# Three moves in a two-block fp32 kernel: most SBUF tiles shifted by 64 bytes, two zeroings put at the head of a GpSimd chain, small VectorE chains cut into more pieces

## Chip, core and metric

The kernel runs as one program on one core of a Trainium2 chip. The metric is device time in microseconds (us) of one execution. The time before is 1152.12 us, the median of three runs (1150.99 to 1152.60).

## What is computed

Two transformer-like blocks over 256 positions of width 1024, in float32, one after the other. The part that matters here is the gated delta rule of the first block (8 heads, 128 wide, chunks of 64 in the reference; the kernel works it with chunks of 128):

```python
def first_block(x, ...):
    h = rmsnorm(x, norm_mix_g[l])
    proj = h @ w_in[l]
    bg, cg, xv, q, k, v, z, a, b, ga, gb = jnp.split(proj, pts, axis=-1)
    y_a = short_conv_branch(bg, cg, xv, conv_a_w[l]) @ w_a_out[l]
    y_b = gdn_branch(q, k, v, z, a, b, ...) @ w_b_out[l]
    mix = jax.nn.sigmoid(ga) * y_a + jax.nn.sigmoid(gb) * y_b
    x = x + mix @ w_o[l]
    h = rmsnorm(x, norm_ffn_g[l])
    x = x + conv_ffn(h, w_up[l], ffn_conv_w[l], w_down[l])
...
def gated_delta_rule_chunked(q, k, v, g, beta):
    G = jnp.cumsum(g, axis=-1)
    decay = jnp.exp(jnp.where(tril, G[..., :, None] - G[..., None, :], -jnp.inf))
    L = jnp.where(strict, jnp.einsum('bnhid,bnhjd->bnhij', k_beta, k) * decay, 0.0)
    sol = lax.linalg.triangular_solve(eye + L, rhs, left_side=True, lower=True)
    ...
    _, o = lax.scan(step, state0, xs)
```

The second block is attention in three dilated groups, a retention branch (a product of decayed scores with values) and a feed-forward part with a squared relu.

## The kernel before

**Jobs and units.** All dense products are cut into jobs of one 1 MB weight load each (`fm_job`, `tm_jobs`, `down_job`, `down2_job`). A job has two halves, called units here. In each unit the main loop does five things in this order: it advances the evacuations (`evs`), it splits the weights of the unit two ahead (`do_split`), it advances the evacuations again, it issues the unit's matmuls, and it advances the side chains (`auxes`) by one `yield` each. So a `yield` more in a side chain puts what follows it one unit later on every engine. The instruction order of each engine is fixed when the program is built; nothing is scheduled later.

**The split.** A float32 product is done as three passes in fp32r: weights are split into H (a ScalarE copy, line 143) and L = raw - H (a VectorE subtraction, line 146), activations likewise into a high and a low tile. A unit of `fm_job` has 24 matmuls (line 334): 128x128 weights from H or L stand still, and 256 columns of an activation tile (Hh, Hl, nh, nl, x2h, ...) are streamed past them. By the code there are 248 such units, 5,952 matmuls of 256 columns into the PSUM tiles named d; 47 of these units come before the inverse described below. `down_job` streams mh and ml past H and L into the PSUM tiles named x (528 matmuls of 256 columns). `tm_jobs` and `down2_job` do it the other way round: 512 columns of H or L are streamed past weights from x2h, x2l (624 matmuls) or mh, ml (384). The retention branch streams 512 columns of vrh, vrl past weights from a `w` tile (lines 325 to 327).

**Where tiles lie.** Each partition of SBUF holds, in this order: the raw weight buffers, the H and L buffers (from byte 41,088 on), the small constants, 15 large buckets of 8 KB (all activation tiles), the temporaries (`w` and others), and the mh/ml buffers. One of the constants is a tile `pad` of `LINE_PAD` floats that nothing reads. In the kernel before H, L, the buckets and mh/ml all start at a multiple of 128 bytes and the `w` tiles start 64 bytes beyond one. The warm-up at the program's start streams 256 columns of zeros whose first byte is 48, 56, 64 and 80 bytes beyond a multiple of 128 (8 matmuls each, list `WARM`), past weights that start at such a multiple.

**The delta rule's side chain.** `gates` computes the decay g with about 25 tiny VectorE operations (128x16 elements). `gdn_decay` sends g through DRAM and back as a 1 MB broadcast into the bucket gam (lines 501 and 502, issued by SP), waits `GAM_Y` units, and turns gam into the decay factors. `gdn_main` forms U (line 565 and what follows), sends its 32x32 diagonal blocks through DRAM into ebd, and queues `subst`. `subst` inverts the 64 small triangles by substitution on partitions 0 to 63: steps 31 to 24 on VectorE, 23 to 1 on GpSimd (line 146, tiles bt and ebd). Then it writes the result and its transpose to DRAM (lines 600 and 602, GpSimd's queue), zeroes the buckets Em, Dm and P (lines 603, 605, 608, GpSimd), waits `SC_Y` units, scatters the blocks into Em and Dm (line 614: block rows 0 and 2 from GpSimd's queue, 1 and 3 from SP's), waits `SC_Z` units and sets `sub_ok`. After that `gdn_main` starts the inverse on TensorE (line 663 reads Dm), between units of dense work. SP also issues all weight loads (line 316), in order; a load waits until its raw buffer is free, and so does everything behind it.

Of the kernel before, what the change touches and what calls it, by code (L numbers as in the profile page):

```python
# [8 lines left out]
I32 = mybir.dt.int32  # L9
# [3 lines left out]
MUL, ADD, SUB = ALU.mult, ALU.add, ALU.subtract  # L13
# [3 lines left out]
D = 1024  # L17
RAW_BUFS = 3
N_BUCKETS = 15
LINE_PAD = 8  # L20
HL_BUFS = 3
W_BUFS = 6
WARM = ([(0, 0, 512, 0)] * 11 + [(128 * i, 1024 + d, 256, i % 2) for d in (12, 14, 16, 20) for i in range(8)])
# [2 lines left out]
DG, DV, DQ = 1, 0, 3  # L26
AT_Y = 5
SQ_Y = 1
GAM_Y = 4
ORDER = ((0,), (1,), (2,))  # L30
D1_Q = 2
SG_Y = {8: 3, 0: 4, 16: 5}
U_Y = 1
SC_Y = 2
SC_Z = 4
EXP1 = 1


# [60 lines left out]
def _build(tc, nc, A, ACT, DVE, POOL, PE, SP, raw_p, hl_p, c_p, b_p, t_p, m_p, s_p, d_p, x_p):  # L99
    uid = [0]  # L100

    def nm(s):
        uid[0] += 1
        return f"{s}{uid[0]}"
# [4 lines left out]
    def alloc(shape, dt=F32, what="bk"):  # L109
        if not free_tags:  # L110
            raise RuntimeError(f"no bucket for {what} at {cur}: {len(tag_of)}")
        tag = free_tags.pop()
        t = b_p.tile([128] + list(shape), dt, tag=tag, name=nm(what))
        tag_of[id(t)] = (tag, t)
        return t

    def free(*ts):
        for t in ts:
            free_tags.insert(0, tag_of.pop(id(t))[0])

    def tmp(tag, shape=(2, 256), dt=F32, bufs=None):
        return t_p.tile([128] + list(shape), dt, tag=tag, name=nm(tag), **({"bufs": bufs} if bufs else {}))

    def cst(name, shape, dt=F32):
        return c_p.tile(list(shape), dt, tag=name, name=name)

    def psx(shape=(512,)):
        t = x_p.tile([128, 512], F32, tag="x", name=nm("x"))
        return shaped(t, shape)
# [12 lines left out]
    def act(out, in_, func, **kw):  # L142
        ACT.activation(out=out, in_=in_, func=func, **kw)  # L143

    def tt(eng, out, a, b, op):
        eng.tensor_tensor(out=out, in0=a, in1=b, op=op)  # L146

    def stt(out, in0, scalar, in1, op0, op1):
        DVE.scalar_tensor_tensor(out=out, in0=in0, scalar=scalar, in1=in1, op0=op0, op1=op1)  # L149

    def ts(out, in0, s1, op0, s2=None, op1=None):
        if s2 is None:
            DVE.tensor_scalar(out=out, in0=in0, scalar1=s1, scalar2=None, op0=op0)
        else:
            DVE.tensor_scalar(out=out, in0=in0, scalar1=s1, scalar2=s2, op0=op0, op1=op1)
# [8 lines left out]
    def pts(out, in0, s1, op0, s2=None, op1=None):  # L164
        if s2 is None:
            POOL.tensor_scalar(out=out, in0=in0, scalar1=s1, scalar2=None, op0=op0)
        else:
            POOL.tensor_scalar(out=out, in0=in0, scalar1=s1, scalar2=s2, op0=op0, op1=op1)

    def rsqrt(y, v, n, steps=3, dve=False):  # L170
        a = tmp(f"nw{n}", (n,))
        DVE.tensor_scalar(out=y.bitcast(I32), in0=v.bitcast(I32), scalar1=-0.5, scalar2=float(0x5F3759DF), op0=MUL, op1=ADD)
        for _ in range(steps):
            if dve:
                tt(DVE, a, y, y, MUL)
                stt(a, a, -0.5, v, MUL, MUL)
                stt(y, a, 1.5, y, ADD, MUL)
                continue
            tt(POOL, a, y, y, MUL)
            tt(POOL, a, a, v, MUL)  # L180
            pts(a, a, -0.5, MUL, 1.5, ADD)
            tt(POOL, y, y, a, MUL)
# [28 lines left out]
    DVE.memset(warm[:, 512:2048].bitcast(F32), 0.0)  # L211
    cst("pad", [128, LINE_PAD])
    eps = cst("epsc", [128, 1])
# [193 lines left out]
    gd = {}  # L407
# [21 lines left out]
    def gates():  # L429
        ps = psx((2, 16))  # L430
        for c in range(2):
            PE.matmul(ps[:, c, :], lhsT=gd["ab"][:, 128 * c:128 * c + 128], rhs=gd["id2"], start=c == 0, stop=c == 1, skip_group_check=True)
        yield
        def sm(n): return cst(n, [128, 2, 8])
        bet, xx, na, u, m, s, s2, p, g = (sm(n) for n in ("bet", "sx", "sna", "su", "smx", "ss_", "ss2", "spp", "gg"))
        gd["bet"], gd["g"] = bet, g
        act(bet, ps[:, :, 8:16], AF.Sigmoid)
        tt(DVE, xx, ps[:, :, 0:8], adt[:, 1:2, :].to_broadcast([128, 2, 8]), ADD)
        stt(na, xx, -1.0, xx, MUL, ALU.min)
        nA = cst("nA", [128, 1, 8])  # L440
        act(nA[:, 0, :], adt[:, 0, :], AF.Exp)
        act(u, na, AF.Exp)
        yield
        ts(m, xx, 0.0, ALU.max)
        ts(s, u, 2.0, ADD)
        DVE.reciprocal(out=s, in_=s)
        yield
        fl = lambda t: t.rearrange("p a b -> p (a b)")
        tt(DVE, fl(s), fl(s), fl(u), MUL)
        tt(DVE, fl(s2), fl(s), fl(s), MUL)  # L450
        ts(fl(p), fl(s2), 1.0 / 17, MUL, 1.0 / 15, ADD)
        yield
        for k in range(6, -1, -1):
            tt(DVE, fl(p), fl(p), fl(s2), MUL)
            ts(fl(p), fl(p), 1.0 / (2 * k + 1), ADD)
            if k in (2, 4):
                yield
        ts(fl(s), fl(s), -2.0, MUL)
        tt(DVE, fl(p), fl(p), fl(s), MUL)
        tt(DVE, fl(p), fl(p), fl(m), SUB)  # L460
        for c in range(2):
            tt(DVE, g[:, c, :], p[:, c, :], nA[:, 0, :], MUL)
        yield
        yield
        yield from gdn_decay()
        yield from gdn_main()

    def gdn_norm_k():
# [15 lines left out]
    def gdn_decay():  # L484
# [17 lines left out]
        SP.dma_start(out=gam.rearrange("p a b -> p (a b)"), in_=gs.rearrange("a b -> (a b)").partition_broadcast(128))  # L502
        for _ in range(GAM_Y):
            yield
# [48 lines left out]
    def gdn_main():  # L553
        ks, sums = gd["ks"], gd["sums"]
        kt0, St = ks[:, 0], ks[:, 1]
        rq, sq = gd["rq"], gd["sq"]
# [24 lines left out]
        def subst():  # L581
            ef = eb.rearrange("p r c -> p (r c)")
            POOL.memset(ef, 0.0)
            POOL.memset(ef[:, 0:1024:33], 1.0)
            for _ in range(3):
                yield
            def step(eng, i):
                w = 32 - i
                t = tmp("bt", (256,))[0:64, 0:i * w].rearrange("p (r c) -> p r c", c=w)
                tt(eng, t, blk[:, 0:i, i:i + 1].to_broadcast([64, i, w]), eb[:, i:i + 1, i:32].to_broadcast([64, i, w]), MUL)  # L590
                tt(eng, eb[:, 0:i, i:32], eb[:, 0:i, i:32], t, SUB)

            for i in range(31, 0, -1):
                step(POOL if i < 24 else DVE, i)
                if i % (2 if 7 < i < 24 else 4) == 0:
                    yield
            for _ in range(SUB_W):
                yield
            gd["Em"], gd["Dm"] = alloc([16, 128], what="Em"), alloc([16, 128], what="Dm")
            POOL.dma_start(out=d2.rearrange("b u r c -> (b u) r c"), in_=eb)  # L600
            POOL.tensor_copy(out=blk, in_=eb.rearrange("p r c -> p c r"))
            POOL.dma_start(out=d3.rearrange("b u r c -> (b u) r c"), in_=blk)
            POOL.memset(gd["Em"], 0.0)
            yield
            POOL.memset(gd["Dm"], 0.0)
            yield
            gd["P"] = alloc([16, 128], what="P")
            POOL.memset(gd["P"], 0.0)
            for _ in range(SC_Y):
                yield  # L610
            for dd, dst in ((d2, gd["Em"]), (d3, gd["Dm"])):
                for b in range(4):
                    bs = slice(32 * b, 32 * b + 32)
                    (POOL, SP)[b % 2].dma_start(out=dst[bs, :, bs], in_=dd[b].rearrange("u r c -> r u c"))
            free(ebd)
            for _ in range(SC_Z):
                yield
            gd["sub_ok"] = True

        auxes.append((subst(), ()))  # L620
        while "q_ok" not in gd:
            yield
# [20 lines left out]
        free(gam, KQ[0])  # L643
        yield
        ts(sq, sq, EPS, ADD)
        rsqrt(rq, sq, 16, dve=True)
        rq2 = cst("rq2", [128, 16])
        ts(rqs, rq, 128 ** -0.5, MUL)
        tt(DVE, rq2, rqs, rqs, MUL)
# [2 lines left out]
        Em, Dm, P = gd["Em"], gd["Dm"], gd["P"]  # L652
# [137 lines left out]
        S["ob"] = (Oh, Ol)  # L790

    jobs.append(Job(load_w("w_in", 0, 8, 7168, 128), ab_mm, ab_evac, halves=1, start=(gates,), split=ab_split))
    for p in range(4):
        fm_job("w_in", 4096 + 256 * p, "x", qkv_evac(K, 8, p), start=(gdn_keys,) if p == 3 else ())
# [871 lines left out]
```

## Time and profile before

| | us |
|---|---|
| median of 3 runs | 1152.12 |
| the profiled execution, its own time | 1150.97 |
| its span, first to last instruction | 1149.2 |
| TensorE busy (matmul) | 1127.2 |
| VectorE busy | 750.5 |
| ScalarE busy | 586.0 |
| GpSimd busy | 241.7 |
| mean granted TensorE clock | 0.991 |

The span is 1.8 us shorter than the execution's own time. Matmuls are pipelined and the ends of their rows are modelled, so the spacing of their starts says more than their durations. In rows, `d<-Hh,L` means: into PSUM tile d, streamed tile Hh, standing weights L. A release in brackets names what ended the idle time ahead of a row.

### The profile page before, as it was taken

Reading aid. Unit: us, or ns where it says so; the run is one execution under the profiler, and the core shown is the slowest. Engines: PE = TensorE matmul, PEld = TensorE weight load, DVE = VectorE, ACT = ScalarE, POOL = GpSimd, SP = SyncE. Lnnn points to the kernel's source line nnn. Section 1 sums busy time; section 2 is a strip of 40 time slices with the busy share of each in tenths; the row PEclk is TensorE's granted clock in tenths of the full one; section 3 lists DMA queues with packets and bytes.
Section 4 is the critical chain, followed back from the end, with each engine's and each line's share of the span. In section 5 each row is a group of like instructions: output and inputs, shape, how many; then the busy total and the mean of one; then the engine's idle time right before and its main releaser. Section 6 shows DMA issues by size and latency. Waiting matters only on the chain.

```text
span 1149.2 us, 20224 instructions
## 1 busy us (share of the span) xinstructions
PE 1127.2 (98%) x8340; PEld 1073.6 (93%) x8340; DVE 750.5 (65%) x1033; ACT 586.0 (51%) x944; POOL 241.7 (21%) x245
## 2 busy tenths in 40 slices
PE   9899897999999999999999999999999999999998
PEld 8899897999999999999878899889999999899997
DVE  4957984344577987778854566556685558655554
ACT  6776253256554444444678554555474445444442
POOL 2565696010401221222200500001340001000000
PEclk9999998999999999999999999999999999999999
DMA  8455366243554555555575544453436555555552
GB/s 258 147 164 186 111 193 174 75 146 112 182 186 150 181 188 183 192 178 178 183 250 190 184 146 147 139 191 113 163 129 220 184 184 168 176 191 189 190 187 74
DMA packets 155087, 194.82 MB, mean 170 GB/s; under 512 B 5678, under 2 KB 132005, under 8 KB 154740
## 3 DMA queue, kind: packets, MB, share of 16 engines
q1 hardware_dynamic: 153888, 191.57, 51.1%
q0 software_dynamic: 912, 1.43, 0.5%
q8 instruction: 65, 1.06, 0.4%
q10 hardware_dynamic: 196, 0.54, 0.1%
q14 instruction: 26, 0.21, 0.0%
HBM read 191.68 MB, written 1.84 MB: 168 GB/s over the span
## 4 chain that ended last, share of the span: by engine, by line
PE 84%; POOL 5%; DVE 4%; ACT 3%; DMA 2%; issue 2%; POOLq 0%; DVEq 0%; ACTq 0%
PE d L334 63%; PE x L334 13%; POOL bt L146 2%; POOL ebd L146 2%; DVE L L146 2%; ACT jk L143 1%; ACT H L143 1%; DVE w L149 1%; DMA Dm<-scr 1%; POOL gam L146 1%; PE x L663 0%; PE x L1181 0%; PE x L1206 0%; DMA scr<-U 0%; DMA xtm<-in_x_dram 0%
## 5 line engine op out<-in xcount | busy, mean ns | idle before, releaser
L146 DVE TENSOR_TENSOR L<-raw,H 128x1024 fp32r<-128x1024 f32 x354 | 443.2, 1258 | 256.8 <-ACT H L143 253.2
L143 ACT ACTIVATE H<-raw 128x1024 fp32r<-128x1024 f32 (+1 forms) x355 | 369.9, 1053 | 205.2 <-PE d L334 152.4
L334 PE MATMUL d<-Hh,L 128*128 128x256 f32 x576 | 82.2, 286 | 6.2 <-DVE L L146 6.2
L334 PE MATMUL d<-Hh,H 128*128 128x256 f32 x576 | 85.6, 292 | 0.7 <-ACT H L143 0.7
L334 PE MATMUL d<-nh,H 128*128 128x256 f32 x608 | 85.9, 283 | 0.0
L334 PE MATMUL d<-nl,H 128*128 128x256 f32 x608 | 85.7, 283 | 0.0
L334 PE MATMUL d<-nh,L 128*128 128x256 f32 x608 | 85.7, 283 | 0.0
L334 PEld LDWEIGHTS d<-Hh,L 128*128 128x128 f32 x576 | 74.7, 193 | 7.4 <-DVE L L146 7.4
L334 PE MATMUL d<-Hl,H 128*128 128x256 f32 x576 | 81.2, 284 | 0.0
L334 PEld LDWEIGHTS d<-nh,H 128*128 128x128 f32 x608 | 79.2, 191 | 1.2
L334 PEld LDWEIGHTS d<-nh,L 128*128 128x128 f32 x608 | 78.6, 192 | 0.0
L334 PEld LDWEIGHTS d<-nl,H 128*128 128x128 f32 x608 | 78.5, 192 | 0.0
L334 PEld LDWEIGHTS d<-Hh,H 128*128 128x128 f32 x576 | 75.2, 194 | 1.4 <-ACT H L143 0.9
L334 PEld LDWEIGHTS d<-Hl,H 128*128 128x128 f32 x576 | 74.9, 193 | 0.0
L334 PE MATMUL d<-H,x2h 128*128 128x512 f32 x208 | 56.9, 396 | 1.0 <-ACT H L143 1.0
L334 PE MATMUL d<-x2h,H 128*128 128x256 f32 x384 | 55.8, 288 | 0.0
L334 PE MATMUL d<-H,x2l 128*128 128x512 f32 x208 | 55.7, 390 | 0.0
L334 PE MATMUL d<-L,x2h 128*128 128x512 f32 x208 | 55.7, 390 | 0.0
L334 PE MATMUL d<-x2h,L 128*128 128x256 f32 x384 | 53.9, 283 | 0.0
L334 PE MATMUL d<-x2l,H 128*128 128x256 f32 x384 | 53.9, 283 | 0.0
L334 PEld LDWEIGHTS d<-x2h,H 128*128 128x128 f32 x384 | 49.8, 190 | 0.6
L334 PEld LDWEIGHTS d<-x2h,L 128*128 128x128 f32 x384 | 49.5, 191 | 0.0
(402 smaller groups left out, 1922.8 us busy)
## 6 DMA issues: line engine op xcount, KB each, us to landing
raw<-in_w_in_dram SPq DMA_DIRECT2D x86, 1024.0 KB, 5.1
raw<-in_w_up_dram SPq DMA_DIRECT2D x38, 1024.0 KB, 5.3
raw<-in_w_down_dram SPq DMA_DIRECT2D x27, 1024.0 KB, 4.8
raw<-in_w_proj_b_dram SPq DMA_DIRECT2D x8, 1024.0 KB, 5.1
raw<-in_w_a_out_dram SPq DMA_DIRECT2D x4, 1024.0 KB, 6.1
raw<-in_w_b_out_dram SPq DMA_DIRECT2D x4, 1024.0 KB, 5.3
raw<-in_w_o_dram SPq DMA_DIRECT2D x4, 1024.0 KB, 6.0
raw<-in_w_out_dram SPq DMA_DIRECT2D x4, 1024.0 KB, 5.2
```

Of the source, the lines that this page charges most:

```text
L143: ACT.activation(out=out, in_=in_, func=func, **kw)
L146: eng.tensor_tensor(out=out, in0=a, in1=b, op=op)
L149: DVE.scalar_tensor_tensor(out=out, in0=in0, scalar=scalar, in1=in1, op0=op0, op1=op1)
L334: PE.matmul(out, lhsT=x if swap else w, rhs=w if swap else x, start=first and ps == 0, stop=last and ps == group[-1] and group is (order o ...
```

## The change

Five edits. `LINE_PAD` goes from 8 to 24 floats, so that every tile behind `pad` moves up by 64 bytes: the buckets and mh/ml now start 64 bytes beyond a multiple of 128, the `w` tiles at a multiple; raw, H and L stay. The zeroing of Em and Dm moves from behind the substitution to its head, with its two `yield`s; `SC_Z` goes from 4 to 6. In `gates` the loop yields at four places instead of two; `GAM_Y` goes from 4 to 2. The reciprocal root of the query norms is written out with a `yield` after each of its three rounds.

```diff
-LINE_PAD = 8
+LINE_PAD = 24
-GAM_Y = 4
+GAM_Y = 2
-SC_Z = 4
+SC_Z = 6
         for k in range(6, -1, -1):
             tt(DVE, fl(p), fl(p), fl(s2), MUL)
             ts(fl(p), fl(p), 1.0 / (2 * k + 1), ADD)
-            if k in (2, 4):
+            if k in (1, 2, 4, 5):
                 yield
...
             POOL.memset(ef, 0.0)
             POOL.memset(ef[:, 0:1024:33], 1.0)
-            for _ in range(3):
-                yield
+            gd["Em"], gd["Dm"] = alloc([16, 128], what="Em"), alloc([16, 128], what="Dm")
+            for k in ("Em", "Dm"):
+                POOL.memset(gd[k], 0.0)
+                yield
+            yield
...
             for _ in range(SUB_W):
                 yield
-            gd["Em"], gd["Dm"] = alloc([16, 128], what="Em"), alloc([16, 128], what="Dm")
             POOL.dma_start(out=d2.rearrange("b u r c -> (b u) r c"), in_=eb)
             POOL.tensor_copy(out=blk, in_=eb.rearrange("p r c -> p c r"))
             POOL.dma_start(out=d3.rearrange("b u r c -> (b u) r c"), in_=blk)
-            POOL.memset(gd["Em"], 0.0)
-            yield
-            POOL.memset(gd["Dm"], 0.0)
-            yield
             gd["P"] = alloc([16, 128], what="P")
...
         ts(sq, sq, EPS, ADD)
-        rsqrt(rq, sq, 16, dve=True)
+        a = tmp("nw16", (16,))
+        DVE.tensor_scalar(out=rq.bitcast(I32), in0=sq.bitcast(I32), scalar1=-0.5, scalar2=float(0x5F3759DF), op0=MUL, op1=ADD)
+        for _ in range(3):
+            tt(DVE, a, rq, rq, MUL)
+            stt(a, a, -0.5, sq, MUL, MUL)
+            stt(rq, a, 1.5, rq, ADD, MUL)
+            yield
```

On VectorE, the end of `gates` (spp and its neighbours are the tiny tiles, L the weight splits that TensorE waits for, w a convolution). Before:

```order
L146 TENSOR_TENSOR spp<-spp,ss_342 128x16
L153 TENSOR_SCALAR spp<-spp 128x16
L146 TENSOR_TENSOR spp<-spp,ss_342 128x16
L153 TENSOR_SCALAR spp<-spp 128x16
L153 TENSOR_SCALAR ss__341<-ss__341 128x16
L146 TENSOR_TENSOR spp<-spp,ss__341 128x16
L146 TENSOR_TENSOR spp<-spp,smx 128x16
L146 TENSOR_TENSOR gg<-spp,nA 128x8 x2
L146 TENSOR_TENSOR L_580<-raw_303,H_579 128x1024
L146 TENSOR_TENSOR L_617<-raw_403,H_616 128x1024
```

In the change:

```order
L146 TENSOR_TENSOR spp<-spp,ss_342 128x16
L153 TENSOR_SCALAR spp<-spp 128x16
L146 TENSOR_TENSOR L_610<-raw_403,H_609 128x1024
L149 SCALAR_TENSOR_TENSOR w_603<-d_535,prm,w_603 128x254 x2
L149 SCALAR_TENSOR_TENSOR w_603<-d_535,prm,w_603 128x253 x2
L146 TENSOR_TENSOR spp<-spp,ss_342 128x16
L153 TENSOR_SCALAR spp<-spp 128x16
L153 TENSOR_SCALAR ss__341<-ss__341 128x16
L146 TENSOR_TENSOR spp<-spp,ss__341 128x16
L146 TENSOR_TENSOR spp<-spp,smx 128x16
L146 TENSOR_TENSOR gg<-spp,nA 128x8 x2
L146 TENSOR_TENSOR L_659<-raw_403,H_658 128x1024
```

The nine tiny operations that stood ahead of L in one run now have a split and a convolution between them, seven remain together, and gg is complete two units later.

On GpSimd, the end of `subst`. Before:

```order
L600 DMA scr_1284<-ebd_1290 64x1024
L601 COPY ebd_1290<-ebd_1290 64x1024
L602 DMA scr_1285<-ebd_1290 64x1024
L603 MEMSET Em_1992 128x2048
L605 MEMSET Dm_1993 128x2048
L608 MEMSET P_2062 128x2048
L614 DMA Em_1992<-scr_1284 32x16x32 x2
L614 DMA Dm_1993<-scr_1285 32x16x32 x2
```

In the change:

```order
L602 DMA scr_1284<-ebd_1290 64x1024
L603 COPY ebd_1290<-ebd_1290 64x1024
L604 DMA scr_1285<-ebd_1290 64x1024
L606 MEMSET P_1999 128x2048
L612 DMA Em_1342<-scr_1284 32x16x32 x2
L612 DMA Dm_1343<-scr_1285 32x16x32 x2
```

Two zeroings are gone from between the substitution's result and its scatters; they now stand right behind lines 583 and 584, ahead of the first substitution step on GpSimd.

On SP, the same place. Before:

```order
L316 DMA raw_2002<-in_w_in_dram 128x8x256
L316 DMA raw_2068<-in_w_a_out_dram 128x8x256
L614 DMA Em_1992<-scr_1284 32x16x32 x2
L614 DMA Dm_1993<-scr_1285 32x16x32 x2
L316 DMA raw_2146<-in_w_a_out_dram 128x8x256
```

In the change:

```order
L316 DMA raw_2005<-in_w_in_dram 128x8x256
L612 DMA Em_1342<-scr_1284 32x16x32 x2
L612 DMA Dm_1343<-scr_1285 32x16x32 x2
L316 DMA raw_2076<-in_w_a_out_dram 128x8x256
L316 DMA raw_2146<-in_w_a_out_dram 128x8x256
```

SP's scatters now stand ahead of the first load of `w_a_out`. The inverse itself (line 663) starts behind the same unit as before, the 48th: two units fewer for the zeroings, two more from `SC_Z`.

## Rows read from the trace of the kernel before

**Rows 1.** The page, part 1: busy time, share of the span, instructions.

```profile
PE 1127.2 (98%) x8340; PEld 1073.6 (93%) x8340; DVE 750.5 (65%) x1033; ACT 586.0 (51%) x944; POOL 241.7 (21%) x245
```

**Rows 2.** Waits of TensorE's matmul queue over the whole span: engine, tile, line, whom it waited for, us in total, times, longest.

```profile
PE x L663 <- DMA Dm<-scr: 7.9, 1, 7.9
PE d L334 <- DVE L L146: 6.2, 6, 2.4
...
```

**Rows 3.** Busy time by stretch: us, then busy (instructions) of PE, PEld, DVE, ACT, POOL, then the granted TensorE clock, DMA share, GB/s.

```profile
188.00:210.00 22.00, 22.00 (x148) 20.81 (x147) 10.78 (x16) 5.47 (x7) 7.95 (x5) 0.79 0.31 97
572.00:975.00 403.00, 402.02 (x2808) 376.63 (x2808) 251.46 (x326) 220.71 (x366) 47.20 (x51) 1.00 0.52 172
```

**Rows 4.** Instructions of TensorE in order of time, around its waits: start us, us, and in brackets the idle time ahead and its releaser.

```profile
40.37 1.22 PE L334 MATMUL d<-Hh,L 128*128 128x256 f32 x8 [0.70 <-DVE L L146]
...
49.08 1.22 PE L334 MATMUL d<-Hh,L 128*128 128x256 f32 x8 [2.27 <-DVE L L146]
...
51.26 2.08 PE L334 MATMUL d<-Hh,H 128*128 128x256 f32 x8
...
138.86 1.89 PE L334 MATMUL d<-Hh,L 128*128 128x256 f32 x8 [2.40 <-DVE L L146]
...
187.40 3.65 PE L663 MATMUL x<-Dm,U 128*128 128x64 f32 x16 [7.92 <-DMA Dm<-scr]
190.80 2.06 PE L334 MATMUL d<-yah,H 128*128 128x256 f32 x8
...
194.09 1.12 PE L334 MATMUL d<-yah,L 128*128 128x256 f32 x8
```

**Rows 5.** Instructions of VectorE in order of time, 36 to 49 us, the end of `gates`.

```profile
44.19 0.16 DVE L146 TENSOR_TENSOR spp<-spp,ss 128x16 f32<-128x16 f32 x1
...
47.81 2.35 DVE L146 TENSOR_TENSOR L<-raw,H 128x1024 fp32r<-128x1024 f32 x2
```

**Rows 6.** Instructions of VectorE and of SP's queue in order of time, 50 to 82 us: the way of gam.

```profile
56.63 0.27 DVE L498 COPY gr<-x 16x128 f32<-16x128 f32 x1
...
58.47 0.34 SPq L502 DMA_DIRECT2D gam<-gs  x1
...
64.11 0.68 DVE L549 COPY ks<-x 128x512 f32<-128x512 f32 x1
...
70.91 1.28 DVE L146 TENSOR_TENSOR gam<-gam,cmats 128x512 f32<-128x512 f32 x2
```

**Rows 7.** Instructions of GpSimd in order of time, 95 to 192 us.

```profile
122.96 0.59 POOL L146 TENSOR_TENSOR bt<-ebd 64x207 f32<-64x207 f32 x1 [8.94 <-DVE ebd L146]
...
172.16 0.54 POOL L602 DMA_DIRECT2D scr<-ebd  x1 [0.30 <-POOL ebd L601]
172.69 1.82 POOL L603 MEMSET Em<- 128x2048 f32 x1
174.43 1.82 POOL L605 MEMSET Dm<- 128x2048 f32 x1
...
179.26 1.29 POOL L614 DMA_DIRECT2D Dm<-scr  x2
```

**Rows 8.** SP's queue in order of time, 163 to 181 us.

```profile
163.06 0.37 SPq L316 DMA_DIRECT2D raw<-in_w_a_out_dram  x1
...
177.22 1.05 SPq L316 DMA_DIRECT2D raw<-in_w_a_out_dram  x2
```

**Rows 9.** DMA issues by tensor: issuing queue, count, KB each, median us from issue to landing.

```profile
raw<-in_w_in_dram SPq DMA_DIRECT2D x86, 1024.0 KB, 5.1
...
raw<-in_w_a_out_dram SPq DMA_DIRECT2D x4, 1024.0 KB, 6.1
...
scr<-ebd POOLq DMA_DIRECT2D x2, 256.0 KB, 2.9
...
Dm<-scr SPq DMA_DIRECT2D x2, 64.0 KB, 2.4
...
Dm<-scr POOLq DMA_DIRECT2D x2, 64.0 KB, 7.4
```

**Rows 10.** The chain that ended last, whole span: start us, us, what. These pieces are gapless runs of matmuls, so length over count is their spacing.

```profile
395.10 11.52 PE d L334 x96
...
406.61 5.70 PE x L334 x48
...
846.66 120.95 PE d L334 x1008
...
1088.83 5.58 PE x L334 x24
```

**Rows 11.** Instructions of TensorE in order of time: the end of the warm-up, 512-column streams past x2l, and the retention product.

```profile
6.16 3.96 PE L271 MATMUL d<-warm 128*128 128x256 f32 x32
9.96 0.27 PE L250 MATMUL d<-cmats,prr 128*128 128x128 f32 x1
...
592.64 1.07 PE L334 MATMUL d<-H,x2l 128*128 128x512 f32 x4
...
596.26 1.07 PE L334 MATMUL d<-L,x2h 128*128 128x512 f32 x4
...
783.22 0.39 PE L325 MATMUL x<-vrh,w 128*128 128x512 f32 x1
...
785.28 0.88 PE L334 MATMUL d<-x2h,H 128*128 128x256 f32 x6
```

## The prediction

> **What bounds the kernel now.** I read the page's busy times first: TensorE's matmul queue is busy for 1127.2 us of the 1149.2 us span, VectorE for 65%, GpSimd for 21% [rows 1]. So almost the whole time is matmul spacing, and a saving is either a wait of TensorE that goes or a closer spacing. The list of TensorE's waits comes next: one of 7.9 us for the DMA into Dm, and 6.2 us in six waits for the weight split L on VectorE [rows 2]. The instructions around them [rows 4] show the waits at 40.4, 49.1, 138.9 and 187.4 us. A wait can also cost clock: 8 matmuls take 2.06 us in the row at 190.80 and 1.12 us in the row at 194.09, where the clock is back. [...] So the five edits split into two groups: the side chains can only change what happens before about 190 us, and the 64 bytes can change the spacing everywhere.
>
> **The change part by part: zeroing.** GpSimd ends the substitution's writes with the DMA at 172.16, zeroes Em, Dm and P, then issues its scatters, Dm's last [rows 7]. The zeroings start 1.74 us apart (172.69, 174.43), so without two of them the Dm scatters issue 3.5 us earlier, at 175.8 instead of 179.26. They read what the DMA of 172.16 writes, and such writes land in 2.9 us [rows 9], at 175.0: that holds nothing back. At their new place the zeroings take 3.5 us of GpSimd while VectorE does steps 31 to 24; GpSimd sits idle there for 8.94 us [rows 7]. That cover is enough, so they cost nothing. If it were gone, they would cost the same 3.5 us and the edit would be void. TensorE's wait ends when the last Dm scatter lands, so the resumption moves by **-3.5 us**.
>
> **Scatter and loads.** GpSimd's Dm scatters take 7.4 us to land, SP's only 2.4 [rows 9]; GpSimd's were issued 2 us behind two 1 MB loads on SP at 177.22 [rows 8]. In the change SP's scatters wait for the data landing at 175.0, and three loads stand right behind, among them the one that used to go at 163.06 [rows 8]. GpSimd's Dm scatters at 175.8 thus still meet loads. I take 7.4 again, which is the row of the same queue beside loads: **0 us**, with a gain of up to 5.0 us if they landed as SP's do. The moved load issues near 175.8 instead of 163.06, lands 6.1 us later [rows 9] at 181.9, and is split some 2.4 us later, if ScalarE's copy takes no more than VectorE's 1.2 us (two L in 2.35 us [rows 5]), by 184.3. Its first matmuls stand behind 16 inverse matmuls of 3.65 us [rows 4] that now start near 183.9, so they would be asked for at 187.6: covered by 3.4 us. If the scatters did land in 2.4 us, this cover would cap the gain at about 4.6.
>
> [...]
>
> **Gates in more pieces.** The tiny operations from 44.19 to 47.8 us push L to 47.81 [rows 5], and TensorE waits 2.27 us for it; the earlier wait of 0.70 us has the same source [rows 4]. With the row at 51.26 (2.08 against 1.12) about 1.0 us of clock, and some 0.3 behind it, hang on the longer one. All of it is 4.3 us. The pieces now stand between splits, but seven operations stay together at the end. The price is that gr, at 56.63, moves two units on, to where the second ks copy stood, 64.11 [rows 6]. The 1 MB gam transfer then issues near 66 instead of 58.47; in before's time its first use, at 70.91, does not move since `GAM_Y` loses two units. A 1 MB load lands in 5.1 us [rows 9], so gam would land near 71: no cover is left, and a late gam holds VectorE and the splits queued behind it, for which TensorE waits. I take **-2.5 us** that reach the scatter chain, between 0 (gam eats it) and -4.3.
>
> **Root in three pieces.** Twelve tiny operations ahead of L cost TensorE the 2.40 us at 138.9 and some clock after [rows 4]. This lies before the wait for Dm, whose end GpSimd's chain sets, not TensorE. What TensorE saves there it waits longer at 187.4: **0 us**, and up to 4 if that chain stopped being the last. So the side chains give -3.5 - 2.5 = -6.0 us, between 0 and -12.5.
>
> **The 64 bytes.** TensorE is busy for 98% of the span [rows 1], so it is on spacing that they can act in bulk. Read from gapless runs: the d products with 256 columns, streamed tile and weights both at a multiple of 128, have 120.95/1008 = 119.99 ns and 11.52/96 = 120.0; the x products past mh, also both at 0, 5.70/48 = 118.75 [rows 10]. The nearest to the new state is the warm-up, streamed 48 to 80 bytes beyond: from 6.16 to 9.96 us 32 matmuls, 118.75 ns [rows 11]. With 512 columns: 226.3 ns past x2l and x2h (592.64 to 596.26, 16 matmuls, both at 0), 5.58/24 = 232.5 past mh [rows 10], and 228.9 in the retention product (783.22 to 785.28, 9 matmuls), whose `w` weights lie 64 bytes off the streamed vr tiles [rows 11]. So where 64 bytes are already in the kernel, 256 columns are 1.25 ns closer than now, and 512 columns 2.6 ns wider than one neighbour and 3.6 closer than the other. For the 512-column products I take 0. For the 4,824 matmuls of 256 columns into d behind the inverse I take the warm-up's row, since it has their shape and the same PSUM pattern: 4,824 x 1.25 ns = **-6.0 us**. The bounds are 0 and -2.5 ns on one side (-12 us), and the retention row's +2.6 ns on the other.
>
> The sum: 1150.97 - 6.0 - 6.0 = 1139.0 for the profiled execution. The median of the runs is 1.15 us above that execution, so I forecast **1140.1 us**.
>
> **The rivals.**
> - *The spacing does not depend on where tiles lie.* Then the 118.75 of the x products is a matter of PSUM tiles, and that of the warm-up of its zeros. For it: x and d differ with both at 0. Against it: the warm-up uses d tiles like the 120 ns runs. Only -6.0 remains: 1146.1. [...]
> - *The 64 bytes widen the spacing, as in the retention row.* At +2.6 ns on 4,824 matmuls of d, 528 of the x products and 1,008 of 512 columns, 6,360 in all, this is +16.5 us, net +10.5: 1162.6, slower than before. It decides from 6.0 us / 6,360 = 0.94 ns per matmul on. For it: that row has exactly the new distance. Against it: its other 512-column neighbour is wider still.
> - *The wait for Dm does not end earlier,* because GpSimd's scatters stay behind the loads that now stand closer, or gam arrives late. Then only the spacing counts: 1146.1. For it: 7.4 against 2.4 us shows how loads hold scatters; against it: they held them before as well.
> - *The scatters land early too:* -4.3 - 3.5 - 4.6 with the spacing's -6.0 gives 1133.7.
>
> **How the numbers follow.** The forecast has 43%, unmoved spacing 24%, wider spacing 15%, an unmoved wait 9%, early scatters 9%. The range 1130 to 1149 takes in all but the wider spacing and the far ends, about 2 in 10. About 0.2% (2.3 us) is what a measurement of this kernel can tell from no change. Faster by more: 43 + 9, 20 of the 24, 6 of the 9 and 1 of the 15, 79%. Within: 4 + 3 + 1 = 8%. Slower: 13%.
>
> **What would show it.** In the profile after, Dm's zeroing stands near 114 to 118 us and no longer near 174; GpSimd's last scatter issues some 6 us earlier and the inverse starts near 181; the wait there may be as long as before. The waits at 40 and 49 us are gone or under 1 us, and none appears at gam near 68. A d run of 1008 matmuls takes 119.7 us instead of 120.95. I am wrong if that run is 120.9 or longer, if line 663 starts after 185, or if a new wait stands behind gam.

## The result and the profile after

| | before | after |
|---|---|---|
| median of 4 runs, us | 1152.30 | 1134.52 |
| range of the runs, us | 1150.99 to 1152.60 | 1133.89 to 1136.21 |
| span of the profiled execution, us | 1149.2 | 1132.1 |
| start of the inverse (line 663, now 667), us | 187.40 | 181.35 |
| from there to the end, us | 961.8 | 950.75 |

The ratio is 0.985, with a 95% interval of 0.9833 to 0.9867: the change makes the kernel 17.8 us faster. The two last lines of the table split the profiled executions' 17.1 us: 6.05 us come before the inverse, 11.05 us behind it. The page's first part, as [rows 1]:

```profile
PE 1111.5 (98%) x8340; PEld 1054.7 (93%) x8340; DVE 754.4 (67%) x1033; ACT 584.8 (52%) x944; POOL 242.0 (21%) x245
```

TensorE's busy time is 15.7 us less for the same 8340 matmuls, and its share is still 98%: it is again the spacing that fills the time. Next TensorE's waits over the whole span, as [rows 2] (waiting tile and line, whom it waited for, us in total, times, longest):

```profile
PE d L334 <- DVE L L146: 6.8, 7, 2.5
PE x L667 <- DMA Dm<-scr: 6.0, 1, 6.0
```

The waits have moved more than they have shrunk. TensorE's instructions around them, as [rows 4]:

```profile
46.12 1.21 PE L334 MATMUL d<-Hh,L 128*128 128x256 f32 x8 [0.65 <-DVE L L146]
...
53.44 1.21 PE L334 MATMUL d<-Hh,L 128*128 128x256 f32 x8 [0.95 <-DVE L L146]
...
77.00 1.22 PE L334 MATMUL d<-Hh,L 128*128 128x256 f32 x8 [1.18 <-DVE L L146]
...
139.34 1.21 PE L334 MATMUL d<-Hh,L 128*128 128x256 f32 x8 [2.50 <-DVE L L146]
...
181.35 3.65 PE L667 MATMUL x<-Dm,U 128*128 128x64 f32 x16 [6.00 <-DMA Dm<-scr]
184.75 2.05 PE L334 MATMUL d<-yah,H 128*128 128x256 f32 x8
```

The waits behind `gates` (0.70 and 2.27 us before) are 0.65 and 0.95 us, and no row of 2.08 us follows. A new wait of 1.18 us stands at 77.00. The 2.40 us behind the root are 2.50 us one unit later. On VectorE the source of the new wait is seen: it stood idle 2.03 us for gam.

```profile
69.40 1.29 DVE L146 TENSOR_TENSOR gam<-gam,cmats 128x512 f32<-128x512 f32 x2 [2.03 <-DMA gam<-gs]
```

GpSimd's instructions, as [rows 7]:

```profile
113.31 1.81 POOL L587 MEMSET Dm<- 128x2048 f32 x1
120.79 0.59 POOL L146 TENSOR_TENSOR bt<-ebd 64x207 f32<-64x207 f32 x1 [5.67 <-DVE ebd L146]
...
170.18 0.55 POOL L604 DMA_DIRECT2D scr<-ebd  x1 [0.30 <-POOL ebd L603]
170.71 1.83 POOL L606 MEMSET P<- 128x2048 f32 x1
...
173.80 1.29 POOL L612 DMA_DIRECT2D Dm<-scr  x2
```

The zeroings lie in idle time, 5.67 us of which are still left, and the Dm scatters follow the last write by 3.62 us instead of 7.10. The gapless runs of the chain that ended last, as [rows 10] (start, us, what):

```profile
381.88 5.45 PE x L334 x48
...
797.73 24.49 PE d L334 x216
...
834.20 118.72 PE d L334 x1008
...
1106.00 5.51 PE x L334 x24
```

Length over count: x past mh with 256 columns 113.5 ns (118.75 before), d 117.8 ns in the long run (120.0 before), but 113.4 in the run of 216, and the 512 columns past mh 229.6 ns (232.5 before). The 512 columns past x2 went the other way, 2.80 us for the 12 matmuls between the first and the last of these rows, 233.3 ns (226.3 before):

```profile
572.42 1.10 PE L334 MATMUL d<-L,x2h 128*128 128x512 f32 x4
573.35 1.10 PE L334 MATMUL d<-H,x2h 128*128 128x512 f32 x4
574.28 1.09 PE L334 MATMUL d<-H,x2l 128*128 128x512 f32 x4
575.22 1.09 PE L334 MATMUL d<-L,x2h 128*128 128x512 f32 x4
```

The sum behind the inverse is thus 4,824 x -2.21 - 528 x 5.25 + 624 x 7.0 - 384 x 2.9 ns = -10.2 us, against -11.05 measured. Three things in the traces are not in it. Over a run of 240, before and after, the 512 columns past x2 widened by 6.3 ns and not 7.0 (228.1 to 234.4), which makes the sum -10.6:

```profile
588.84 54.74 PE d L334 x240
...
576.84 56.26 PE d L334 x240
```

The d runs at 113.3 to 113.5 ns (the 216, 48 each at 677.09 and 693.14, and 24 at 792.95) bring some 1.5 us more. And the first 24 matmuls of d behind the wait for Dm, before and after, took 0.7 us longer: the granted clock over them was 0.67 before (190.80 to 195.20 us) and 0.54 after (184.75 to 189.70).

```profile
191.04 4.17 PE d L334 x24
...
185.00 4.88 PE d L334 x24
```

Together that is -11.4 us; the last 0.3 us stay open.

### The profile page after: what moved, and what is told of

Same layout as the page of the kernel before. It is cut to its first block, busy times and chain, and to the rows that moved or that the text cites. A ratio compares the mean times of both kernels' runs of the same rounds, so it can differ in the third digit from the quotient of the medians.

```text
span 1132.1 us, 20217 instructions
## 1 busy us (share of the span) xinstructions
PE 1111.5 (98%) x8340; PEld 1054.7 (93%) x8340; DVE 754.4 (67%) x1033; ACT 584.8 (52%) x944; POOL 242.0 (21%) x245
## 4 chain that ended last, share of the span: by engine, by line
PE 83%; POOL 5%; DVE 5%; DMA 2%; ACT 2%; issue 2%; DVEq 0%; ACTq 0%; POOLq 0%
PE d L334 62%; PE x L334 13%; POOL ebd L146 2%; POOL bt L146 2%; DVE L L146 2%; ACT jk L143 1%; ACT H L143 1%; DVE w L149 1%; DMA Dm<-scr 1%; PE x L667 0%; PE x L1185 0%; PE x L1210 0%; DMA scr<-U 0%; DMA xtm<-in_x_dram 0%; PE x L669 0%
## 5 line engine op out<-in xcount | busy, mean ns | idle before, releaser
L334 PE MATMUL d<-Hh,H 128*128 128x256 f32 x576 | 82.9, 285 | 0.6 <-ACT H L143 0.6
L334 PEld LDWEIGHTS d<-Hh,H 128*128 128x128 f32 x576 | 72.6, 188 | 1.1 <-ACT H L143 0.8
L143 ACT ACTIVATE w<-w 128x512 f32<-128x512 f32 (+1 forms) x35 | 21.7, 619 | 51.8 <-POOL w L146 19.9
```

The lines of the kernel that those rows point to most:

```text
L334: PE.matmul(out, lhsT=x if swap else w, rhs=w if swap else x, start=first and ps == 0, stop=last and ps == group[-1] and group is (order o ...
```

## The experiments

All times are medians of their runs, and ratios are to the kernel before, run on the same chip. Numbers 8, 11 and 12 are single runs; only the spacing in their traces is read.

**1. The pad alone.** The kernel before with

```diff
-LINE_PAD = 8
+LINE_PAD = 24
```

> The kernel before with LINE_PAD 24 and nothing else. Theory (the spacing follows from where the tiles lie): the same spacing as in the changed kernel, 117.75 ns for d, 113.5 ns for x past mh, 233 ns for 512 columns past x2, 229 past mh. Behind the inverse that is 4,824 x -2.25, 528 x -5.2, 624 x +6.3 and 384 x -3 ns, -10.8 us, and some 1.8 us more because TensorE reaches the delta rule sooner (about 800 matmuls of d before 104 us): 1139.7 us. [...]

Measured: 1141.43 us, ratio 0.9913 (0.9896 to 0.9929). The spacing is that of the changed kernel: 117.8 ns for d (118.72 us for the run of 1008) and 113.5 for x past mh (5.45 us for 48). From the inverse to the end it is 949.8 us, 12.0 less than before. The inverse did not start sooner but 2.4 us later: GpSimd's scatters were issued 1.2 us later and took 8.7 us to land instead of 7.4 (the last one 8.60 instead of 7.36).

```profile
189.79 3.65 PE L663 MATMUL x<-Dm,U 128*128 128x64 f32 x16 [9.70 <-DMA Dm<-scr]
```

So the pad makes the spacing without any moved instruction. My expectation that TensorE would also be earlier at the delta rule fell: ahead of 190 us it waits for L (2.42 us at 48.91 and 2.61 at 140.12, each a little longer than before), and what the spacing gives there is waited off.

**2. The moves alone.** The changed kernel with `LINE_PAD = 8`.

> The changed kernel with LINE_PAD back at 8: the side-chain edits alone. By the prediction's terms (-3.5 zeroing, -2.5 gates): 1146.3 us, inverse at 181.4. Rival: the 2 us by which the substitution starts sooner come from the closer spacing and not from the gates: 1148.5 us, inverse at 183.3 to 183.9. Rival (the moved instructions made the spacing): 1134.5 us and 117.75 ns.

Measured: 1145.54 us, ratio 0.9946 (0.9931 to 0.9961). The prediction's sum of the side chains, -6.0 us, is met (-6.1 between the medians, -5.2 between the profiled executions), and 120.0 ns are back. The rival, by which the closer spacing brought part of those 6 us, falls. From the inverse to the end it is 961.8 us, as before.

```profile
182.21 3.65 PE L667 MATMUL x<-Dm,U 128*128 128x64 f32 x16 [4.60 <-DMA Dm<-scr]
```

**3. Zeroing back at its old place.** The changed kernel with

```diff
-            gd["Em"], gd["Dm"] = alloc([16, 128], what="Em"), alloc([16, 128], what="Dm")
-            for k in ("Em", "Dm"):
-                POOL.memset(gd[k], 0.0)
-                yield
-            yield
+            for _ in range(3):
+                yield
...
+            gd["Em"], gd["Dm"] = alloc([16, 128], what="Em"), alloc([16, 128], what="Dm")
...
             POOL.dma_start(out=d3.rearrange("b u r c -> (b u) r c"), in_=blk)
+            POOL.memset(gd["Em"], 0.0)
+            yield
+            POOL.memset(gd["Dm"], 0.0)
+            yield
```

and `SC_Z = 4`.

> The changed kernel with the zeroing of Em and Dm back behind the substitution and SC_Z back at 4. Theory: the zeroings stand on GpSimd's chain, +3.5 us: 1138.0, inverse near 184.9. Rival (GpSimd's last scatters are held by the loads anyway, whenever they are issued): under +1 us, 1134.5 to 1135.5, the scatters' landing shorter by what their issue is later.

Measured: 1139.46 us, ratio 0.9893 (0.9878 to 0.9908), 4.9 us above the changed kernel. The inverse starts 4.84 us later:

```profile
186.19 3.65 PE L669 MATMUL x<-Dm,U 128*128 128x64 f32 x16 [9.33 <-DMA Dm<-scr]
```

On GpSimd the last write stands 0.67 us later than in the changed kernel and the Dm scatters follow it by 7.12 us instead of 3.62:

```profile
170.85 0.54 POOL L602 DMA_DIRECT2D scr<-ebd  x1 [0.30 <-POOL ebd L601]
...
177.97 1.29 POOL L614 DMA_DIRECT2D Dm<-scr  x2
```

The zeroings cost their own 3.5 us; the other 1.3 us are the later start and a landing 0.7 us longer. The rival (the loads hold the scatters whenever they are issued) falls.

**4. Gates as before.** The changed kernel with

```diff
-            if k in (1, 2, 4, 5):
+            if k in (2, 4):
...
-GAM_Y = 2
+GAM_Y = 4
```

> The changed kernel with two yields in gates and GAM_Y 4, as before. By the prediction's term: +2.5 us, 1137.0, waits of 0.7 and 2.3 us at some 40 and 49 us back, with 1 us of clock. Rival (what the pieces save is given back where gam arrives late, a wait of 1.18 us at 77 us): 1134.5 to 1135.2, the inverse no later than 181.9.

Measured: 1137.82 us, ratio 0.988 (0.9866 to 0.9895). The inverse starts 2.17 us later than in the changed kernel, and the waits are the old ones:

```profile
40.51 1.21 PE L334 MATMUL d<-Hh,L 128*128 128x256 f32 x8 [0.86 <-DVE L L146]
...
49.23 1.18 PE L334 MATMUL d<-Hh,L 128*128 128x256 f32 x8 [2.42 <-DVE L L146]
...
183.52 3.65 PE L667 MATMUL x<-Dm,U 128*128 128x64 f32 x16 [5.33 <-DMA Dm<-scr]
```

So the pieces in `gates` are worth 2.2 us, gam's new wait included. The remaining time over the changed kernel, in the profiled execution, lies where this edit has nothing to do: x past mh ran at 5.65/48 = 117.7 ns here and at 113.5 in the changed kernel, with the same addresses, 528 x 4.2 ns = 2.2 us. Like the d run of 216 in the changed kernel, this is a sign that one layout holds two spacings.

```profile
383.71 5.65 PE x L334 x48
```

**5. H and L moved as well.** The changed kernel with `LINE_PAD = 8` and

```diff
+    hl_p.tile([128, 16], F32, tag="hpad", name="hpad", bufs=1)
```

ahead of H and L, so that every tile lies where the change puts it, but 64 bytes no longer separate it from the weights.

> The changed kernel with H and L 64 bytes further too (a pad ahead of them, LINE_PAD back at 8), so that streamed tile and weights are as far apart as before the change, and every tile's own place is that of the changed kernel. Theory distance: spacing as before, 120.0 (d), 118.6 (x past mh), 227 and 232 ns (512 columns past x2, mh), 1145.5 us. Rival own place of the streamed activation tile: 117.4 and 113.3 ns stay for 256 columns, 1135 us or so.

Measured: 1146.20 us, ratio 0.9952 (0.9936 to 0.9969), and the old spacing, 118.75 and 119.9 ns:

```profile
384.40 5.70 PE x L335 x48
390.10 11.51 PE d L335 x96
```

So the streamed tile's own place does not make the spacing; the distance between it and the standing weights does, which number 8 bears out at every distance that it tries (with 256 columns within 0.1 ns when both tiles move 64 bytes).

**6 and 7. Other pads.** The changed kernel with `LINE_PAD = 40` (128 bytes more than before the change) and with `LINE_PAD = 16` (32 more).

> The changed kernel with LINE_PAD 40: everything behind the pad 128 bytes further than before the change instead of 64. Theory line (only the place within 128 bytes counts): spacing as before, 120.0, 118.6, 227 and 232 ns, 1145.5 us. Rival period of 512 bytes (d and x past mh differed before at the same place in 128 bytes): other numbers, d at the distance of 384 that mh had, 118.6 ns, 1140 us.

> The changed kernel with LINE_PAD 16: 32 bytes instead of 64. Theory line, all or nothing (any place off the weights' line counts alike): 117.4 and 113.3 ns, 233 ns past x2, 1134.5 us. Rival in proportion: half of it, 118.7 and 116 ns, 1140 us. Rival 64 only: as before, 1145.5 us.

Measured: 1143.73 us, ratio 0.993 (0.9915 to 0.9945), and 1135.95 us, ratio 0.9867 (0.9853 to 0.9882). From the chain of the first (`LINE_PAD = 40`):

```profile
383.71 5.75 PE x L334 x48
389.46 11.39 PE d L334 x96
...
986.53 5.76 PE d L334 x48
```

At 128 bytes more, d (11.39/96 = 118.6) takes the spacing that x past mh had before, and x past mh (119.8) that of d. So 128 bytes are not the period. But d did not keep one value: in later runs such as the one at 986.53 it had 120.0. At 32 bytes d runs at 116.7 ns (11.20 us for 96) and x past mh at 118.75 (5.70 us for 48), which none of the three expectations had. That the time, 1135.95 us, comes near the 1134.5 of the first of them is luck: d is closer than it said and x past mh is not closer at all.

**8 and 11. A map.** Extra runs in the warm-up, nothing else: 32 matmuls of 256 columns of zeros (16 of 512) at each distance.

```diff
+MAP = ([(256, 16 * w, r) for w in (0, 1) for r in range(0, 512, 32)] + [(512, 0, r) for r in range(0, 512, 32)])
...
+        for n, wo, rel in MAP:
+            for i in range(32 if n == 256 else 16):
+                w0 = 64 + wo + 128 * (i % 8)
+                m0 = 1216 + wo + rel // 4
```

In number 11 the steps are 8 bytes, up to 256.

> The changed kernel with LINE_PAD 8 and a longer warm-up: runs of 32 matmuls with 256 columns (16 with 512) of zeros, the streamed bytes 0 to 480 bytes from the weights modulo 512 in steps of 32, the 256-column ones twice, with all of it 64 bytes further the second time. Theory distance with a period of 512: the spacings that the kernels show come again, about 120 at 256, 118.6 at 384, 117.4 at 320, 113.3 at 448, and 227, 233, 232, 229 with 512 columns at 256, 192, 128, 64, the same the second time. Theory line: two values only, alike at 0, 128, 256 and 384. Rival (neighbouring engines' traffic sets it): about one value at all places here. The time is longer by the added matmuls, some 185 us.

> The long warm-up with steps of 8 bytes over 256 bytes. Theory: 192 is a narrow best place for 256 columns, as its neighbours at 160 and 224 with 117.3 and 118.3 ns say, and 0 the one for 512 columns; between the steps of 32 the spacing goes from one to the other. Rival: lower spacings lie between the steps of 32.

Measured (1325.98 and 1387.54 us): mean ns between the starts of matmuls in the trace, without the first 8 (4) of a run, by the distance from the weights to the streamed tile in bytes; below them the kernels' gapless runs at the same distance modulo 256, each product with one of its values (number 12 says more on those distances that hold two).

```
distance           0      32     64     96     128    160    192    224
256 columns     120.0  117.9  117.7  120.1  118.9  117.3  113.3  118.3
  d             120.0  116.7  117.8         118.6
  x past mh     119.8                       118.75 118.75 113.5
512 columns     227.1  233.3  229.2  233.5  233.0  234.0  233.6  232.8
  past x2       226.3                                     233.3
  past mh                     229.6         232.5
```

At 256 to 480 bytes the same values come again (256 columns: within 0.1 ns, 512: within 0.5), and so they do with everything 64 bytes further (256 columns, within 0.1 ns). The kernels' runs in the table differ from the zeros by 1.5 ns at most, at 160. Over the 480 bytes tried the period is 256, and the rival by which other engines' traffic makes the spacing falls: in the stretch of the first 1024 matmuls of number 8 the other engines hardly work (columns as in [rows 3]: VectorE 0.28 us, ScalarE and GpSimd nothing, clock 1.00, DMA share 0.07).

```profile
10.70:131.00 120.30, 120.30 (x1023) 120.30 (x1022) 0.28 (x1) 0.00 (x0) 0.00 (x0) 1.00 0.07 21
```

With steps of 8 bytes and 256 columns, 15 of the 16 odd multiples of 8 gave 119.9 to 121.2 ns, so 192 is narrow (184: 120.0, 200: 120.0); but 112 gave 113.9, which I had not expected, and 32 gave 116.8 this time.

**9. The best place of the map.** The changed kernel with `LINE_PAD = 56` and 128 bytes ahead of mh, so that d and x past mh both have a distance of 192, and the 512 columns one of 64 (as before, modulo 256 and from the weights to the streamed tile).

```diff
+    m_p.tile([128, 32], F32, tag="mpad", name="mpad", bufs=1)
```

> The changed kernel with the buckets 128 bytes further (LINE_PAD 56) and the mh/ml buffers 128 bytes further than that, so that both lie 192 bytes from H and L modulo 256; past x2 the 512-column streams then lie 64 from their weights. Theory distance modulo 256 (the long warm-up): 113.3 ns for d instead of 117.75, x past mh stays at 113.3, 229.2 ns instead of 233.2 past x2, 229 past mh stays: 4,824 x -4.45 + 624 x -4.0 = -24 us, 1110.5 us. Rival (TensorE outruns the loads or the splits once it is closer): waits of TensorE behind the inverse of 5 us and more in sum, 1116 us or more. Rival (the map of zeros in a quiet start does not carry over): 1134.5.

Measured: 1129.65 us (1126.66 to 1132.29), ratio 0.9805 (0.9785 to 0.9825): 4.9 us under the changed kernel, where 24 were expected. TensorE waits behind the inverse for two short times only, 0.9 us each for an H and for sr, so that rival falls too. The chain of its profiled execution shows what is missing: the spacing of 113.4 is there in some runs (24.50/216), and 117.8 in most, x past mh among them, which had 113.5 in the changed kernel at the same distance.

```profile
381.12 5.65 PE x L335 x48
386.77 11.31 PE d L335 x96
...
796.14 24.50 PE d L335 x216
...
832.62 118.72 PE d L335 x1008
```

**10. The same with all scatters on SP.**

```diff
-                    (POOL, SP)[b % 2].dma_start(out=dst[bs, :, bs], in_=dd[b].rearrange("u r c -> r u c"))
+                    SP.dma_start(out=dst[bs, :, bs], in_=dd[b].rearrange("u r c -> r u c"))
```

> The run before it in this list with all eight scatters on SP, ahead of the loads of w_a_out. Theory (GpSimd's last Dm scatter lands in 6.8 us only because a load stands ahead of or beside it): Dm's scatters land by 2.9 us after 174.5, the inverse starts near 177.5 instead of 181.3, -3.5 us. Rival (the loads are late in turn, and TensorE waits for the first L of w_a_out instead): under 1 us.

Measured: 1125.68 us (1123.63 to 1128.11), ratio 0.9775 (0.9756 to 0.9793), the fastest of all. Two things are mixed in it. The scatters into Dm land early as the theory said (a median of 2.4 us after their issue, where GpSimd's last one took 7.08 in number 9), and the inverse starts 4.1 us sooner than in number 9, but the rival is in part right as well: the load behind them is late (it went at 176.63 us and took 6.02), and TensorE gives back 3.51 us waiting for the first H of `w_a_out`. Once both kernels run without waits, number 10 is 1.75 us ahead (the same d run starts at 306.47 and at 308.22 us).

```profile
178.10 2.24 PE L668 MATMUL x<-Dm,U 128*128 128x64 f32 x16 [3.48 <-DMA Dm<-scr]
183.85 2.07 PE L335 MATMUL d<-yah,H 128*128 128x256 f32 x8 [3.51 <-ACT H L143]
```

The rest of the gain in the profiled execution is spacing again: with no address changed, the runs from 396 to 537 us are at 113.3 ns (5.44/48, 10.88/96) and not at 117.8 as in number 9, while the run of 1008 is at 117.8 in both. What picked the spacing in either is not shown.

```profile
395.88 5.44 PE x L335 x48
401.31 10.88 PE d L335 x96
...
825.02 118.72 PE d L335 x1008
```

**12. Two rhythms at one distance.** The warm-up again, with one matmul of 16 to 256 columns ahead of each run of 24:

```diff
+MAP = [(rel, n) for rel in (0, 64, 128, 192) for n in range(16, 272, 16)]
...
+            PE.matmul(wps[2][:, 0:n], lhsT=warm[:, 64:192], rhs=warm[:, m0:m0 + n], start=True, stop=True, skip_group_check=True)
+            for i in range(24):
```

> A longer warm-up again (the changed kernel, LINE_PAD 8): at distances of 0, 64, 128 and 192 bytes modulo 256, 16 runs of 24 matmuls with 256 columns of zeros, each behind one matmul of 16, 32, ... 256 columns that disturbs the rhythm. Theory (one distance can hold two rhythms, and the last disturbance picks which): at 64 and 192 some runs settle at 113.3 ns and others at 117.75, by the length of the matmul ahead; at 0 all settle at 120.0. Rival (each distance has one spacing, and what differs in the kernel comes from other engines' traffic): the same spacing in all 16 runs of a distance, 117.75 at 64 and 113.3 at 192. The time is longer by the added matmuls, some 190 us.

Measured (1332.02 us): at 192 the last half of a run has 113.3 to 113.4 ns behind matmuls of 64, 112, 144, 192, 208 and 224 columns, and 117.7 to 117.8 behind the other ten. At 0 it is 120.0 in all sixteen, at 64 it is 117.7 to 117.8 in all sixteen, at 128 between 118.3 and 120.0. Three of the 192 runs (with their modelled ends, some 0.2 us longer than 24 spacings):

```profile
187.21 2.90 PE L279 MATMUL d<-warm 128*128 128x256 f32 x24
189.95 0.26 PE L277 MATMUL d<-warm 128*128 128x224 f32 x1
190.05 2.90 PE L279 MATMUL d<-warm 128*128 128x256 f32 x24
192.78 0.27 PE L277 MATMUL d<-warm 128*128 128x240 f32 x1
192.89 2.99 PE L279 MATMUL d<-warm 128*128 128x256 f32 x24
```

The theory holds at 192 in that one distance has two lasting spacings. That the matmul ahead picks one is likely but not shown: each length was tried once, in rising order, so a length and its place in the order cannot be told apart. It fell at 64, where all sixteen gave the same spacing and none 113.3; in the changed kernel some runs at that distance had the closer one (113.4 ns over the 216 matmuls at 797.73, 113.5 over 48 at 677.09), so 64 holds two as well, and what leads to the closer one there is open.

## Why the prediction was right, and which of its terms was mis-sized

The forecast of 1140.1 us was 5.6 us above the measured 1134.52. The side chains brought what was forecast; most of the difference is the term for the 64 bytes.

**Side chains.** The term of -6.0 us measured -6.1 (number 2), and 6.05 by the start of the inverse in the change itself. Zeroing off the chain: 3.5 us forecast, and 3.5 us is what the distance from the last write to the Dm scatters gained; the cover on GpSimd held, with 5.67 us left. Landing: 0 forecast, 0.6 us found (7.36 to 6.77 for the last one). Gates: 2.5 forecast, 2.2 measured (number 4). The price named for them was there: gam landed at 69.37, no cover was left, and 1.18 us of waiting stand at 77.00. By the prediction's own signs a new wait behind gam would have shown it wrong; the wait came, though the 2.2 us are what is left with it paid. Root: 0 forecast; the wait of 2.4 us only moved one unit on, to 139.34, and lies ahead of the wait for Dm either way; no run takes this edit back alone. The first load of `w_a_out` was forecast to land at 181.9 and landed at 182.15, and TensorE did not wait for it. For early scatters the prediction named a cap of about 4.6 us without saying how it follows from a cover of 3.4. In number 10, where all the scatters stand ahead of that load, they do land early, the load is late and 3.5 of 4.1 us are given back at once; 1.75 us were left by 306 us.

**The 64 bytes: -6.0 us forecast, about -11 measured.** The sign was right, and the pad alone made it (number 1); the size was not right. The step that mis-sized it is "I take the warm-up's row, since it has their shape": that row averages four places, 48, 56, 64 and 80 bytes, and in the fine map these are 118.4, 120.1, 117.8 and 120.1 ns. The eight matmuls at 64 bytes alone, from the start of the second to the end of their run, have 117.7 ns start to start in the trace of the kernel before (the first spacing is 123), and would have given -2.3 ns and not -1.25. Measured are -2.21, which for d makes -10.7 us instead of -6.0. The second step, "for the 512-column products I take 0", netted +2.8 to +3.3 us (+3.9 to +4.4 past x2, -1.1 past mh), since the two move to different distances; and the x products past mh, which I left out behind the inverse, brought -2.8.

**The rivals.** Unmoved spacing falls with number 1: the pad alone brings 10 us. Number 5 says the same from the other side: it differs from the changed kernel only in where H and L lie, and has 120.0 ns back (120.95 us for the run of 1008). Wider spacing came true for one product, the 512 columns past x2, which moved to a distance of 192 (233.3 ns). It did not for d, and the 512 columns past mh, which took the retention row's spacing (229.6 ns against its 228.9), came closer: the widths have maps of their own. For the wait for Dm, which ended 6.05 us earlier, it is open whether the shift of the tiles Em and Dm cost anything. In the changed order GpSimd's last Dm scatter landed in 6.87 us without the shift (number 2) and in 6.77 with it. In the old order it landed in 7.36 us before and in 7.45 with the shift in number 3, but in 8.60 in number 1, where SP's scatters into Dm took no longer than before (a median of 2.4 us both times).

**What stays open.** Why a period of 256 bytes, and why these values, no run here tells. Nor was it tried to bring the d products of number 9 into the closer spacing on purpose. If all of them went from 117.8 to 113.3 ns it would be, as an estimate from these two, 4,824 x 4.45 ns, some 21 us, of which number 10 has a part.

## What to carry to other kernels

When TensorE is busy nearly all the time (98% here), read spacing as length over count of gapless runs, for each kind of product and each distance between streamed tile and weights; never average a test run over several places. Map the distances in one kernel with a few hundred extra matmuls of zeros before choosing a layout, and let each width vote with its count, since a place that is good for 256 columns can be bad for 512 (at 192, 113.3 ns was the least of the steps of 32, and 233.6 stood against 227.1 at 0). Try each distance behind different matmuls: the map had only 113.3 ns at 192, and the kernel laid out by it ran at 117.8 for the most part and gained 4.9 us of 24. Before crediting an edit, look at whether gapless runs elsewhere changed their spacing: two spacings at one layout made 2.2 us between the traces of number 4 and the change, and some 5.7 us between those of numbers 9 and 10, with no address changed; that can be taken for the worth of an edit. Whether they also make the spread among the runs of one kernel (5.6 us in number 9) is not shown, as one run of each kernel was traced.

## What was not expected of the hardware

The spacing of fp32r matmuls depended on the distance of the two tiles modulo 256 bytes, over the 480 tried: 113.3 to 120.1 ns with 256 columns and 226.6 to 234.0 with 512, in steps of 32. At a distance of 192 two spacings, 113.3 and 117.8 ns, each lasted over hundreds of matmuls and across job borders (in number 10 from 396 to 537 us and in the run of 1008); in number 12 the one that followed changed with the length of a single matmul ahead, six of sixteen lengths leading to the closer one, each tried once. Two spacings also stood at 64 (113.4 and 117.8) and at 128 (118.6 and 120.0). The runs of the kernel laid out for 192 spread over 5.6 us (1126.66 to 1132.29), those of the kernel before over 1.6.
